# Hymba step on one core: a contiguous copy of the query for the residue blocks of two chunks, the last recurrence unit's first steps ahead of the scores, another order of tile pools, later merge turns

## The chip, the cores and the metric

The kernel runs on one core of a Trainium2 chip. The metric is the device time of one execution in microseconds (us), the median of several runs. A profiled execution of the same program gives the trace; its times are counted from its first instruction. TensorE is called PE (its weight loads PEld), VectorE DVE, ScalarE ACT, GpSimd POOL, and the queue that issues most DMAs SP.

## The reference, cut to what matters

One layer of a hybrid decoder over 2048 prompt tokens and 8x4 sample tokens, in float32:

```
a = rmsnorm(x);  [qa|fa|ia|ga|qb|kb|vb] = a @ w_in
h = x + concat(HGRN2(qa,fa,ia,ga), DilatedAttn(qb,kb,vb)) @ w_o
h = h + ConvFFN(rmsnorm(h))
h = h + sigmoid(rmsnorm(h) @ w_ple_gate) * (p @ w_ple_proj);   y = rmsnorm(h)
```

HGRN2 is a gated linear recurrence with 4 heads of 128: `S_t = diag(f_t) S_{t-1} + k_t v_t^T`, `o_t = S_t^T q_t`, then a per-head rmsnorm and a gate. The attention has 8 heads of 64; each query reads the last 129 positions of its sub-sequence for the dilations 1, 4 and 16 (windows 128, 512, 2048), and the three parts are put together by their softmax maxima and sums. The sample tokens do the same against a state and a cache of 2048 positions. The outputs are y for prompt and sample, the new states, and the caches.

## The kernel before, in words

The program is one long list of instructions that a tile framework puts in order: within each engine it orders by priority and by a simulated timeline, allocates the tiles, and sets the semaphores. Only PE in the attention stage runs in the order of the code (`manual_schedule`). Three stages follow each other.

**Projections** (0 to about 831 us). `in_phase` computes all of `a @ w_in` in two blocks of tokens; weights and tokens are split into a high and a low part, and each product is three matmuls (L344 to L346). The last group is the keys: each 128 tokens are scaled (L357), rotated (L318 to L321), turned by four transposes (L367), copied (L372) and stored in `kT_d`. Beside the second block, seven of the eight recurrence units run (`hgrn_unit`, two heads and 512 tokens each).

**Attention** (about 831 to 1212 us). Two generators are stepped in turns. `main` is `attn_phase`, `side` is `others()`: the eighth recurrence unit with `apart=True` (more yields), then the sample's attention, then the sample's recurrence. The loop at the end of the kernel steps `main` once a turn, and `side` once a turn up to turn 27 and every second turn later. A step is what lies between two `yield`s; what is stepped by `first` has a higher priority on the engines that the framework orders.

`attn_phase` goes over 4 head pairs p. For each it has two dilation groups: `di` 0 takes the tokens by residue mod 4 (a block is a chunk c of 512 tokens and a residue r), with keys of chunks 0 to c; `di` 1 takes 128 consecutive tokens, with their own and the previous 128 keys. Chunks have 4 blocks. A block of one or two key tiles is one *unit* of work for both heads, a block of three or four is two units. There are 40 units per pair and 160 in all. Pair 3 alternates the groups chunk by chunk. In turn x:

- `Unit.scores` of unit x: two matmuls per head (L797 with the high part of the keys `kH`, L798 with the low part `kL`), weights `lhsT` from `qS`, 128 columns. For `di` 0 these columns are every fourth element of `qS`, for `di` 1 they are consecutive. Keys of `di` 0 are 128(c+1) wide. The scores lie in one of two PSUM tiles `S`; DVE adds the mask and takes the minimum (L802), ACT takes the exponential (L803) into `P`.
- in every odd turn, `turned` for units x-3 and x-2 (transposes L810, copy L812 on DVE or ACT into `pt`) and `sums` for units x-7 and x-6 (`weighted`, matmuls with the values, L822; copy L872).
- what `at(x, ...)` has put down for the turn: `stage` (loads of q and k, L681, SP), `stack` (POOL rounds q, L148, and writes the rest of the rounding into the other half, L692; ACT copies k by residue, L695; POOL takes its rest, L696), `values_chunk` (L717, L720), and the steps of `merge`.

`merge` joins the two groups of a chunk: at +0 it loads statistics (L728), at +2 DVE takes a minimum (L736), POOL a difference (L737), ACT an exponential (L738); at +3 POOL and DVE (L740 to L743, a reciprocal on DVE at L742); at +4 PE transposes the coefficients (L746), ACT copies (L748), SP stores and loads them spread out (L749, L753); at +8 POOL multiplies (L758); at +9 DVE adds (L760; POOL for pair 3) and SP stores the result in `mix_d`.

`hgrn_unit`, in steps: loads and two products; the diagonal (L460 on PE, L461 on DVE); three double levels, each with operands (L469, L474, L476), products (L484) and results (L423, L496) head by head; the last level (L516); transposes (L529); the state (L541, L545) and the outputs (L552, L553); the norm (`rsqrt_small`, L100 to L105), its product (L567), and the final transposes (L574).

The tiles of the attention lie where the projections' tiles lay, so each waits for the last reader of what lay there. The pools are opened in the order `pps` (PSUM of `side`), then `a_d` (stage), `a_r` (`qS`, `kH`, `kL`), `a_w` (mask, values, `P`, `pt`, `cf`, `o0`, `o1`), `a_s`, and the PSUM pools of scores, sums and transposes.

**Trunk** (about 1212 us to the end): output projection, ConvFFN and embeddings, nearly all matmuls of three terms (L142 to L144).

Of the kernel before, what the change touches and what calls it, by code (L numbers as in the profile page):

```python
# [11 lines left out]
F32 = mybir.dt.float32  # L12
# [35 lines left out]
def hymba_step_kernel(ctx: ExitStack, tc: tile.TileContext, I: dict, O: dict):  # L48
# [44 lines left out]
    def f32(ap):  # L93
        return ap.bitcast(F32)
# [341 lines left out]
    def hgrn_unit(u, heads, S, ld, wk, sp, plv, po, pms, msk, apart=False):  # L436
# [99 lines left out]
        for i, h in enumerate(heads):  # L536
# [6 lines left out]
            for c in range(4):  # L543
                s = sp.tile([128, 128], F32, name=f"S{h}", bufs=6)
                V.scalar_tensor_tensor(s, chain[-1], t["D"][:, c:c + 1], pu[:, 128 * c:128 * c + 128],  # L545
                                       op0=ALU.mult, op1=ALU.add)
                chain.append(s)
# [15 lines left out]
        if apart:  # L563
            yield
        for i, h in enumerate(heads):
            o = st[h]["o"]
            V.tensor_mul(o, o, r[:, 4 * i:4 * i + 4].rearrange("p (c x) -> p c x", x=1).to_broadcast([128, 4, 128]))  # L567
        if apart:
            yield
        for i, h in enumerate(heads):  # L570
# [10 lines left out]
    def hgrn_sample(hp, pps):  # L581
# [13 lines left out]
        G.tensor_mul(E, q, f)  # L595
        yield
        at = hp.tile([NS, 4, NS], F32, name="hsat")
# [41 lines left out]
        ahead = [state_in(0), state_in(1)]  # L639
        yield  # L640
        for bb in range(8):
# [31 lines left out]
    def attn_phase(spare, rest):  # L673
# [11 lines left out]

        def stack(c, q, k):
            cs = slice(512 * c, 512 * c + 512)
            js = slice(128 * c, 128 * c + 128)
            split = "p (i r) -> p r i"
            for hh in range(2):  # L690
                round_g(qS[:, hh, cs], q[:, hh])
                G.tensor_sub(qS[64:, hh, cs], q[64:, hh], f32(qS[64:, hh, cs]))  # L692
            for hh in range(2):
                t = k[:, hh].rearrange(split, r=4)
                A.copy(kH[:, hh, :, js], t)  # L695
                G.tensor_sub(kL[:, hh, :, js], t, f32(kH[:, hh, :, js]))  # L696

        first = stage(0, 0, [t[:, :1024].rearrange("p (h t) -> p h t", h=2) for t in spare])
        yield
        dp, rp, wk, sm, pS, pA, pT = rest()  # L700


        qS = rp.tile([128, 2, SEQ], F32R, name="qS")
        kH = rp.tile([128, 2, 4, 512], F32R, name="kH")
        kL = rp.tile([128, 2, 4, 512], F32R, name="kL")
        mask = wk.tile([128, 768], F32, name="mask", bufs=1)
        SP.dma_start(mask, I["amask"])
        stack(0, *first)
        yield
# [16 lines left out]
        def merge(p, c, parts, both):  # L726
# [23 lines left out]

            cf = wk.tile([128, 2, 512], F32, name="cf", bufs=2)
            for h in range(2):
# [10 lines left out]
        class Block:  # L763


            def __init__(self, p, di, c, r):
                self.p, self.di, self.c, self.r = p, di, c, r
                self.pt = {}
                if di == 0:
                    self.q = lambda hh: qS[:, hh, 512 * c + r:512 * c + 512:4]  # L770
                    self.nk = c + 1
                    self.k = lambda t, hh: t[:, hh, r, :128 * c + 128]
                    self.v = [(n, r) for n in range(c + 1)]
                else:
                    b = 4 * c + r
                    self.q = lambda hh: qS[:, hh, 128 * b:128 * b + 128]
                    self.nk = 2 if b else 1
                    self.k = lambda t, hh: t[:, hh].rearrange("p r (n i) -> p n r i", i=32)[:, b + 1 - self.nk:b + 1]
                    self.v = [(x // 4, x % 4) for x in range(b + 1 - self.nk, b + 1)]
# [3 lines left out]
        class Unit:  # L783
# [5 lines left out]
            def scores(self, both):  # L789
# [4 lines left out]
                s = pS.tile([128, 512], F32, name="S")  # L794
                self.pe = wk.tile([128, 512], F32, name="P", bufs=6)
                for i, hh in enumerate(self.heads):
# [8 lines left out]
            def turned(self, on_act):  # L805
# [3 lines left out]
                for i in range(n):  # L809
                    PE.transpose(pt[:, i], self.pe[:, 128 * i:128 * i + 128], ident)  # L810
                out = wk.tile([128, 4, 128], F32, name="pt", bufs=8)
                (A.copy if on_act else V.tensor_copy)(out[:, :n], pt[:, :n])  # L812
# [33 lines left out]
        for p in range(4):  # L846
            for c in range(4):
# [6 lines left out]
                elif c:  # L854
                    at(x - 12, lambda c=c: staged.append(stage(0, c)))
                    at(x - 6, lambda c=c: stack(c, *staged.pop(0)))
                for di in range(2):
# [5 lines left out]
        def sums(u, x):  # L863
# [5 lines left out]
            if bl.r == 3:  # L869
                p, di, c = bl.p, bl.di, bl.c  # L870
                o = wk.tile([128, 512], F32, name=f"o{di}", bufs=5)
                A.copy(o.rearrange("p (i b) -> p b i", b=4) if di == 0 else o.rearrange("p (b i) -> p b i", b=4), acc)  # L872
# [4 lines left out]
                else:  # L877
                    merge_at([x + d for d in (0, 2, 3, 4, 8, 9)], p, c, (outs[c], o), bl.both)

        for x in range(n + 19):  # L880
            if x < n:
# [715 lines left out]
    S = []  # L1597
    for h in range(4):
        s = sp.tile([128, 128], F32, name=f"S{h}", bufs=6)
        G.memset(s, 0.0)  # L1600
        S.append(s)
# [3 lines left out]
    for x in in_phase(1, *args, plv, po):  # L1605
# [5 lines left out]
        else:  # L1611
            first(side, 2 if main else 1)
    first(side, 1000)
    in_st.close()
    pool = pools(attn_st)
    pps = pool("s_ps", 1, space=PSUM)
    rest += (pool("a_d", 2), pool("a_r", 1), pool("a_w", 3), pool("a_s", 3),
             pool("a_pS", 2, space=PSUM), pool("a_pA", 2, space=PSUM), pool("a_pT", 2, space=PSUM))
    step(main, 1)
# [12 lines left out]
    side = others()  # L1632
    with tc.manual_schedule(engines={mybir.EngineType.PE}):
        for turn in itertools.count(1):
            if not step(main, 1):
# [163 lines left out]
```

## Time and profile before

| | us |
|---|---|
| runs of the kernel before | 3019.55, 3015.72, 3021.38 (median 3019.55) |
| the profiled execution: its own time | 3014.84 |
| its span, first to last instruction | 3013.0 |
| PE busy in the span | 2926.5 (97%) |
| DVE, ACT, POOL busy | 2191.6 (73%), 1304.5 (43%), 667.9 (22%) |
| attention stage | about 831 to 1212 |

A row of a timeline has the start, the duration, the engine, the line, the operation, what it writes and reads, its shape and count, and in brackets how long the engine stood idle before it and what released it. Matmuls are pipelined, so the time between the starts of two of them says more than the duration of one. A row of the windows has the busy time of PE, PEld, DVE, ACT and POOL in a stretch, then the granted TensorE clock (1.00 is full), the busy share of the DMA engines, and GB/s. A row of the waits has who waited for whom, us in all, how often, and the longest.

### The profile page before, as it was taken

Reading aid. Unit: us, or ns where it says so; the run is one execution under the profiler, and the core shown is the slowest. Engines: PE = TensorE matmul, PEld = TensorE weight load, DVE = VectorE, ACT = ScalarE, POOL = GpSimd, SP = SyncE. Lnnn points to the kernel's source line nnn. Section 1 sums busy time; section 2 is a strip of 40 time slices with the busy share of each in tenths; the row PEclk is TensorE's granted clock in tenths of the full one; section 3 lists DMA queues with packets and bytes.
Section 4 is the critical chain, followed back from the end, with each engine's and each line's share of the span. In section 5 each row is a group of like instructions: output and inputs, shape, how many; then the busy total and the mean of one; then the engine's idle time right before and its main releaser. Section 6 shows DMA issues by size and latency. Waiting matters only on the chain.

```text
span 3013.0 us, 52001 instructions
## 1 busy us (share of the span) xinstructions
PE 2926.5 (97%) x18639; PEld 2738.0 (91%) x18639; DVE 2191.6 (73%) x4761; ACT 1304.5 (43%) x2824; POOL 667.9 (22%) x780
## 2 busy tenths in 40 slices
PE   8999999999978989999999999999999999999998
PEld 8977789987767667999999999999999999999997
DVE  7666868884466557568988889766769777777777
ACT  5333423231156665334444444544444544444443
POOL 1443222221134553102443431000001000000000
PEclk9999999999989999999999999999999999999999
DMA  5898533342248996766666568677778777778873
GB/s 174 311 337 309 198 103 110 104 134 95 91 115 243 303 246 194 260 225 222 227 209 194 191 198 300 231 250 252 245 231 311 242 245 244 257 248 290 272 274 131
DMA packets 328579, 664.08 MB, mean 220 GB/s; under 512 B 46400, under 2 KB 114112, under 8 KB 326528
## 3 DMA queue, kind: packets, MB, share of 16 engines
q1 hardware_dynamic: 291472, 472.65, 48.4%
q0 software_dynamic: 33264, 121.13, 12.6%
q10 hardware_dynamic: 3584, 66.98, 6.1%
q8 instruction: 147, 2.41, 0.3%
q14 instruction: 112, 0.92, 0.1%
HBM read 513.69 MB, written 213.92 MB: 241 GB/s over the span
## 4 chain that ended last, share of the span: by engine, by line
PE 72%; issue 9%; DVE 7%; DMA 7%; ACT 2%; POOL 2%; SPq 1%; DVEq 0%; POOLq 0%; ACTq 0%
PE mm L142 16%; PE mm L144 16%; PE mm L143 16%; PE mm L346 2%; PE mm L344 2%; PE mm L345 2%; PE lv L484 2%; PE acc L822 2%; PE S L797 1%; PE PT L810 1%; PE S L798 1%; DMA draw<-in_w_down_dram 1%; DMA xr<-in_xT_dram 1%; DVE h L1291 1%; DMA wd_d<-dw 1%
## 5 line engine op out<-in xcount | busy, mean ns | idle before, releaser
L143 PE MATMUL mm<-w 128*128 128x348 f32 (+3 forms) x3636 | 1166.1, 321 | 1.1 <-DVE w L1435 0.7
L142 PE MATMUL mm<-w 128*128 128x348 f32 (+3 forms) x3508 | 1109.7, 323 | 15.2 <-ACT s L1233 5.8
L144 PE MATMUL mm<-w 128*128 128x348 f32 (+3 forms) x3508 | 1117.4, 321 | 1.3 <-DVE w L181 1.3
L143 PEld LDWEIGHTS mm<-w 128*128 128x128 f32 x3636 | 684.3, 188 | 3.8 <-DVE w L1067 1.8
L142 PEld LDWEIGHTS mm<-w 128*128 128x128 f32 x3508 | 656.5, 188 | 23.6 <-ACT s L1233 8.5
L144 PEld LDWEIGHTS mm<-w 128*128 128x128 f32 x3508 | 659.0, 188 | 2.6 <-DVE w L181 1.8
L181 DVE TENSOR_TENSOR w<-raw,w 128x512 fp32r<-128x512 f32 x586 | 421.9, 725 | 170.3 <-ACT w L180 165.3
L180 ACT CAST w<-raw 128x512 fp32r<-128x512 f32 x586 | 360.6, 621 | 402.8 <-PE mm L144 293.1
L1275 POOL DMA_DIRECT2D w<-wd_d x231 | 123.8, 536 | 906.2 <-PE mm L144 800.6
L1291 DVE TENSOR_TENSOR h<-h,mm 128x348 f32<-128x348 f32 (+1 forms) x504 | 248.4, 509 | 45.9 <-PE mm L144 44.4
L803 ACT ACTIVATE P<-P,st 128x256 f32<-128x256 f32 (+3 forms) x256 | 134.1, 526 | 87.5 <-DVE st L802 85.9
L802 DVE CUSTOM_DVE_ANT_0 P<-S,mask 128x256 f32<-128x256 f32 (+3 forms) x256 | 105.0, 449 | 73.1 <-PE S L798 50.1
L1233 ACT COPY s<-mm 128x348 f32<-128x348 f32 (+1 forms) x198 | 87.9, 444 | 158.1 <-PE mm L144 157.8
L345 PE MATMUL mm<-wl,xh 128*128 128x512 f32 x352 | 140.7, 400 | 1.1 <-DVE wl L267 1.1
L344 PE MATMUL mm<-wh,xh 128*128 128x512 f32 x352 | 140.6, 403 | 0.0
L346 PE MATMUL mm<-wh,xl 128*128 128x512 f32 x352 | 140.3, 399 | 0.0
L142 PE MATMUL mm<-xh,wh 128*128 128x384 f32 (+2 forms) x384 | 125.7, 332 | 8.6 <-ACT xh L242 5.1
L143 PE MATMUL mm<-xl,wh 128*128 128x384 f32 (+2 forms) x384 | 126.9, 333 | 0.8 <-DVE xl L243 0.8
L144 PE MATMUL mm<-xh,wl 128*128 128x384 f32 (+2 forms) x384 | 125.5, 330 | 1.5 <-DVE wl L267 1.4
L267 DVE TENSOR_TENSOR wl<-wraw,wh 128x512 fp32r<-128x512 f32 x104 | 86.3, 851 | 34.0 <-POOL wh L148 28.9
L181 DVE TENSOR_TENSOR dw<-draw,dw 128x512 fp32r<-128x512 f32 x77 | 69.4, 909 | 55.8 <-ACT dw L180 55.0
L797 PE MATMUL S<-kH,qS 128*128 128x256 f32 (+3 forms) x256 | 97.7, 396 | 8.2 <-DVE st L802 7.3
(348 smaller groups left out, 5155.0 us busy)
## 6 DMA issues: line engine op xcount, KB each, us to landing
w<-wd_d POOLq DMA_DIRECT2D x231, 512.0 KB, 5.6
wd_d<-dw SPq DMA_DIRECT2D x77, 512.0 KB
out_sk_dram<-in_cache_k_dram ACTq DMA_DIRECT2D x56, 584.0 KB
out_sv_dram<-in_cache_v_dram ACTq DMA_DIRECT2D x56, 584.0 KB
raw<-in_w_gate_dram SPq DMA_DIRECT2D x110, 256.0 KB
raw<-in_w_up_dram SPq DMA_DIRECT2D x110, 256.0 KB
wraw<-in_w_in_dram SPq DMA_DIRECT2D x104, 256.0 KB
raw<-w_gate_d SPq DMA_DIRECT2D x88, 256.0 KB
```

The costliest lines, as they stand in the source:

```text
L142: PE.matmul(ps, lhsT=wh, rhs=xh, start=first, stop=False, skip_group_check=read)
L143: PE.matmul(ps, lhsT=wh, rhs=xl, start=False, stop=False, skip_group_check=read)
L144: PE.matmul(ps, lhsT=wl, rhs=xh, start=False, stop=last, skip_group_check=read)
L180: A.copy(w[:, 0], raw)
L181: V.tensor_sub(w[:, 1], raw, f32(w[:, 0]))
L344: PE.matmul(ps, lhsT=xh[k][:, js], rhs=wh, start=k == 0, stop=False)
L345: PE.matmul(ps, lhsT=xh[k][:, js], rhs=wl, start=False, stop=False)
L346: PE.matmul(ps, lhsT=xl[k][:, js], rhs=wh, start=False, stop=k == NK - 1)
L797: PE.matmul(s[:, w * i:w * i + w], lhsT=bl.q(hh), rhs=bl.k(kH, hh), start=True, stop=False)
L803: A.activation(pe, pe, AF.Exp, bias=mn, scale=-1.0, accum_out=st[:, bl.r, hh, 0:1])
L1275: G.dma_start(t, wd_d[p][n - 1])
L1291: V.tensor_add(o, o, acc[m][:, :H])
```

## The change

1. A new tile `q4` holds the query of chunks 0 and 1 ordered by residue. `stack` fills it with a DVE copy per head for c < 2, and the `di` 0 blocks of these chunks take their weights from it. Chunks 2 and 3 go on reading `qS` in steps of four.
2. For pair 0, the remainders of chunks 0 and 1 (two of q, two of k each) are computed by DVE instead of POOL.
3. Eight steps of `side` are taken ahead of the first turn. With `apart`, the recurrence unit has two more yields around its norm; the sample's recurrence has one more at its start and one less before its states. In all `side` has two more steps.
4. Pools are opened in another order: `a_r` (with `q4`), `a_w`, `a_d`, and a new `a_o` for `o0`, `o1` and `cf`; the PSUM of scores and sums comes before that of `side`.
5. Buffers: `S` of the recurrence 6 to 5, `P` 6 to 5, `pt` 8 to 6.
6. The merge's last three steps move from +4, +8, +9 to +8, +11, +12, and the loop has two more turns.

```diff
@@ hgrn_unit
-                s = sp.tile([128, 128], F32, name=f"S{h}", bufs=6)
+                s = sp.tile([128, 128], F32, name=f"S{h}", bufs=5)
...
         r = rsqrt_small(sp, v.rearrange("p h c -> p (h c)"), [128, 8])
         if apart:
             yield
+            yield
         for i, h in enumerate(heads):
             o = st[h]["o"]
             V.tensor_mul(o, o, r[:, 4 * i:4 * i + 4].rearrange("p (c x) -> p c x", x=1).to_broadcast([128, 4, 128]))
         if apart:
+            yield
             yield
@@ hgrn_sample
         G.tensor_mul(E, q, f)
-        yield
+        for _ in range(2):
+            yield
...
         ahead = [state_in(0), state_in(1)]
-        yield
@@ attn_phase
-        def stack(c, q, k):
+        def stack(c, q, k, E=G):
...
             for hh in range(2):
                 round_g(qS[:, hh, cs], q[:, hh])
-                G.tensor_sub(qS[64:, hh, cs], q[64:, hh], f32(qS[64:, hh, cs]))
+                E.tensor_sub(qS[64:, hh, cs], q[64:, hh], f32(qS[64:, hh, cs]))
+                if c < 2:
+                    V.tensor_copy(q4[:, hh, :, js], f32(qS[:, hh, cs]).rearrange(split, r=4))
             for hh in range(2):
                 t = k[:, hh].rearrange(split, r=4)
                 A.copy(kH[:, hh, :, js], t)
-                G.tensor_sub(kL[:, hh, :, js], t, f32(kH[:, hh, :, js]))
+                E.tensor_sub(kL[:, hh, :, js], t, f32(kH[:, hh, :, js]))
...
-        dp, rp, wk, sm, pS, pA, pT = rest()
+        dp, rp, wk, ok, sm, pS, pA, pT = rest()
         qS = rp.tile([128, 2, SEQ], F32R, name="qS")
+        q4 = rp.tile([128, 2, 4, 256], F32R, name="q4")
...
-        stack(0, *first)
+        stack(0, *first, V)
...
-            cf = wk.tile([128, 2, 512], F32, name="cf", bufs=2)
+            cf = ok.tile([128, 2, 512], F32, name="cf", bufs=2)
...
-                    self.q = lambda hh: qS[:, hh, 512 * c + r:512 * c + 512:4]
+                    self.q = lambda hh: (q4[:, hh, r, 128 * c:128 * c + 128] if c < 2 else
+                                         qS[:, hh, 512 * c + r:512 * c + 512:4])
...
-                self.pe = wk.tile([128, 512], F32, name="P", bufs=6)
+                self.pe = wk.tile([128, 512], F32, name="P", bufs=5)
...
-                out = wk.tile([128, 4, 128], F32, name="pt", bufs=8)
+                out = wk.tile([128, 4, 128], F32, name="pt", bufs=6)
...
-                    at(x - 6, lambda c=c: stack(c, *staged.pop(0)))
+                    at(x - 6, lambda c=c: stack(c, *staged.pop(0), V if c == 1 else G))
...
-                o = wk.tile([128, 512], F32, name=f"o{di}", bufs=5)
+                o = ok.tile([128, 512], F32, name=f"o{di}")
...
-                    merge_at([x + d for d in (0, 2, 3, 4, 8, 9)], p, c, (outs[c], o), bl.both)
+                    merge_at([x + d for d in (0, 2, 3, 8, 11, 12)], p, c, (outs[c], o), bl.both)
...
-        for x in range(n + 19):
+        for x in range(n + 21):
@@ the body
-        s = sp.tile([128, 128], F32, name=f"S{h}", bufs=6)
+        s = sp.tile([128, 128], F32, name=f"S{h}", bufs=5)
...
     pool = pools(attn_st)
+    ar, aw, ad, ao = pool("a_r", 1), pool("a_w", 3), pool("a_d", 2), pool("a_o", 5)
+    rest += (ad, ar, aw, ao, pool("a_s", 3), pool("a_pS", 2, space=PSUM), pool("a_pA", 2, space=PSUM))
     pps = pool("s_ps", 1, space=PSUM)
-    rest += (pool("a_d", 2), pool("a_r", 1), pool("a_w", 3), pool("a_s", 3),
-             pool("a_pS", 2, space=PSUM), pool("a_pA", 2, space=PSUM), pool("a_pT", 2, space=PSUM))
+    rest.append(pool("a_pT", 2, space=PSUM))
     step(main, 1)
...
     with tc.manual_schedule(engines={mybir.EngineType.PE}):
+        first(side, 1)
+        step(side, 7)
         for turn in itertools.count(1):
```

## The prediction

> **What bounds the kernel now.** I read the page first, then the windows of the attention stage, then its waits and timeline engine by engine, because everything the change touches lies there.
>
> ```profile
> span 3013.0 us, 52001 instructions
> PE 2926.5 (97%) x18639; PEld 2738.0 (91%) x18639; DVE 2191.6 (73%) x4761; ACT 1304.5 (43%) x2824; POOL 667.9 (22%) x780
> 840.00:860.00 20.00, 13.20 (x57) 11.84 (x55) 10.00 (x41) 12.54 (x30) 14.81 (x14) 0.63 1.01 256
> 860.00:880.00 20.00, 16.40 (x122) 14.42 (x122) 18.96 (x56) 12.03 (x35) 7.20 (x7) 1.00 0.23 54
> 920.00:940.00 20.00, 17.07 (x145) 13.99 (x145) 16.32 (x58) 14.58 (x43) 12.32 (x18) 0.84 0.95 316
> 940.00:956.00 16.00, 16.00 (x125) 12.14 (x121) 6.17 (x32) 9.74 (x32) 6.97 (x7) 1.00 1.09 270
> 1026.00:1050.00 24.00, 23.99 (x175) 18.09 (x174) 10.69 (x47) 13.36 (x45) 6.07 (x8) 0.93 1.08 275
> ```
>
> PE is the bound: only 86.5 us of the span are left to it, so a gain must come from PE's pauses in this stage, from stretches at a lower clock (0.63, 0.84), or from matmuls that take longer than they need. The last two windows hold the first two chunks of pairs 1 and 2: PE is full there, and DVE has 9.8 of 16 us free. Between 860 and 880 it is DVE that is full (18.96 of 20).
>
> **The query copy.** Start to start tells what a score matmul costs.
>
> ```profile
> 940.60 0.40 PE L797 MATMUL S<-kH,qS 128*128 128x128 f32 x1
> 940.83 0.40 PE L798 MATMUL S<-kL,qS 128*128 128x128 f32 x1
> 899.52 0.28 PE L797 MATMUL S<-kH,qS 128*128 128x128 f32 x1
> 899.64 0.27 PE L798 MATMUL S<-kL,qS 128*128 128x128 f32 x1
> 1038.39 0.39 PE L797 MATMUL S<-kH,qS 128*128 128x256 f32 x1
> 1038.62 0.40 PE L798 MATMUL S<-kL,qS 128*128 128x256 f32 x1
> 1194.87 0.29 PE L798 MATMUL S<-kL,qS 128*128 128x256 f32 x1
> 1194.99 0.29 PE L797 MATMUL S<-kH,qS 128*128 128x256 f32 x1
> ```
>
> The rows at 940 and 1038 have weights from every fourth element and follow at 0.23 us, at width 128 and at 256; those at 899 and 1194 have consecutive weights and follow at 0.12. The width doesn't matter, the step does: the weight load sets the pace, and `q4` saves 0.115 us a matmul. Chunks 0 and 1 have 4 residues x 2 heads x 2 key parts = 16 matmuls each, 32 a pair, 128 in all: 14.7 us, of which 3.7 belong to pair 0 (counted in the start below) and 11.0 to pairs 1 to 3. The Trainium skill says otherwise: "TensorE: Matmul & The Clock Gate", section "LDWEIGHTS (loading the stationary operand)", has a load time that depends on the number of columns alone; by that the copy would gain nothing, and the time would be 3011. The rows at one width differ in nothing but the step, so the measurement decides, and that case gets no chance of its own.
>
> Does PE keep the 11.0? The DMA engines are full in both windows (1.09, 1.08), and the sample's key loads already end last sometimes:
>
> ```profile
> PE s L928 <- DMA skt<-in_kT_d_dram: 5.1, 2, 2.8
> ```
>
> If these loads set the pace, the 7.4 us of pairs 1 and 2 come back as waits, and 3.7 are left. I take 8, between 3.7 and 11.0 and a little nearer to the upper end, since PE is at 16.00 of 16 and 23.99 of 24 in the two windows, with no wait for a DMA in them.
>
> The copy adds 16 DVE instructions of 128x512. No row shows DVE reading in steps of four; the nearest are DVE's copy of this size, and ACT's casts with and without the step.
>
> ```profile
> L812 DVE COPY pt<-PT 128x512 f32<-128x512 f32 x80 | 53.2, 683 | 2.4 <-PE PT L810 2.4
> L695 ACT CAST kH<-stage 128x512 fp32r<-128x512 f32 x30 | 32.7, 1140 | 21.3 <-DMA stage<-kT_d 16.5 <-PE S L797 4.7
> L180 ACT CAST w<-raw 128x512 fp32r<-128x512 f32 x6 | 3.2, 610 | 0.0
> ```
>
> So 0.68 us, or by ACT's ratio 1140/610 up to 1.28; I take 0.7, the same engine. That is 11 us of DVE time (up to 20). For pairs 1 to 3 it lies in DVE's free time; only its place in DVE's queue costs, below. I put 2 us on PE, between 0 and the rival's price.
>
> **The start (831 to 880).**
>
> ```profile
> 830.85 0.39 PE L346 MATMUL mm<-wh,xl 128*128 128x512 f32 x1
> 835.63 1.09 PE L367 MATMUL ms<-c_ident,ev 128*128 128x128 f32 x4 [3.95 <-DVE ev L321]
> 839.56 3.72 PE L460 MATMUL s<-hq,hF 128*128 128x128 f32 x16
> 847.72 0.50 PE L797 MATMUL S<-kH,qS 128*128 128x128 f32 x1 [4.44 <-DVE st L802]
> 859.23 0.89 PE L484 MATMUL s<-hM,hF 128*128 128x192 f32 x4 [1.64 <-DVE at L496]
> 865.87 1.84 PE L484 MATMUL s<-hM,hF 128*128 128x192 f32 x8
> 841.43 0.53 SPq L707 DMA_DIRECT2D mask<-in_amask_dram  x1
> 847.15 0.29 DVE L802 CUSTOM_DVE_ANT_0 P<-S,mask 128x128 f32<-128x128 f32 x1 [4.85 <-DMA mask<-in_amask_dram]
> 826.26 0.22 DVE L319 TENSOR_TENSOR rb<-ev,c_rope 128x64 f32<-128x64 f32 x1
> 832.52 1.30 DVE L319 TENSOR_TENSOR rb<-ev,c_rope 128x64 f32<-128x64 f32 x1
> ```
>
> Projections end at 831.2. The last rotation takes longer than the same line did six us earlier (1.30 for 0.22), and PE waits 3.95. Then the scores stop for the mask, issued on SP only at 841.43, landed at 847.15: PE idles 4.44 and its clock falls. With the pools by time of need, mask and `qS` lie where tiles are read before the very last matmul, so the mask no longer stands behind the second chunk's stage loads. The eight steps taken ahead are the diagonal and the first double level: L460 (3.72 at the low clock, about half at full), L484 for two heads (twice 1.84), with two PE waits of about 1.6 as at 859.23, and DVE's steps between: about 9 us of work that needs neither mask nor `qS`, its loads and operands being long there. They replace the pauses, and PE alone could gain 12 to 15 us.
>
> DVE can't. From 840 to 880 it has 29 us of work in 40 (10.00 and 18.96), and it gets eight remainders and four copies more, 12 x 0.7 = 8 us, a part of it before 840. Some 5 us stay free, and it can't be packed fully, since each L802 waits for scores. I take 5 for the start, pair 0's share of the copy included, with ends 0 and 10.
>
> **The norm of the unit.**
>
> ```profile
> 921.44 1.12 PE L574 MATMUL s<-c_ident,at 128*128 128x128 f32 x4 [5.10 <-DVE at L567]
> 913.52 1.47 DVE L101 TENSOR_SCALAR rs_y<-rs_i 128x8 int32<-128x8 int32 x1
> 920.29 0.17 DVE L104 SCALAR_TENSOR_TENSOR rs_t<-rs_t,o_v 128x8 f32<-128x8 f32 x1
> 907.80 1.20 POOL L148 TENSOR_SCALAR qS<-stage 128x512 fp32r<-128x512 f32 x2 [32.00 <-PE S L798]
> ```
>
> The norm is step 28, its transposes step 30: turns 28 and 32. With the extra yields the transposes are step 32, and with eight steps ahead these are turns 20 and 24: four turns apart as before. But turn 28 falls beside pair 1's `stack` (from turn 31), where POOL works after 32 idle us and DVE's small steps take 1.47 instead of 0.17. Turns 20 to 24 lie in POOL's idle stretch. Eleven steps at 0.2 end in about 2.5 us, the transposes no longer wait, and the 5.10 goes. In the window after it the clock is 0.84: 3 us lost in 20, half of which I count. Gain 6.5, ends 0 and 8.
>
> **The merge.**
>
> ```profile
> 1113.46 0.27 PE L746 MATMUL PT<-c_ident,w 128*16 128x128 f32 x1 [3.54 <-DVE pt L812]
> 1111.10 0.20 DVE L742 RECIPROCAL mn<-mn 128x8 f32<-128x8 f32 x1 [4.68 <-POOL mn L741]
> 1109.70 1.20 POOL L148 TENSOR_SCALAR qS<-stage 128x512 fp32r<-128x512 f32 x2 [5.54 <-DMA stage<-qT_d]
> ```
>
> The big wait at L746 comes from a late stage load: POOL stands at L148, POOL's steps of the merge stand behind it, DVE stands at L742, and the L802s behind that. ACT's cast of the same chunk's keys waits likewise. Of this chain only L746 moves; L742 stays at +3. The next scores and exponentials are as late as before, so I count 1 us, with ends 0 and 4. POOL's products three turns after the transposes instead of four meet their loads sooner; POOL mostly waits there anyway, at no cost.
>
> **Buffers.** Six `pt`, five `P` and five `S` hold exactly what is alive: `pt` of turn x takes the place of a unit summed in turn x-2, `P` that of one turned by x-2, and a state chain has five tiles. All were read on PE before. Cost 0; if a copy is late by a turn, it waits under one turn of PE work, about 2 us.
>
> **The end.** `side` has 94 steps instead of 92 and a lead of 8, so it ends some 12 turns earlier; its PE work isn't lost, only moved. The pair at the end is exposed:
>
> ```profile
> 1204.90 3.47 POOL L758 TENSOR_TENSOR o<-o,cf 128x512 f32<-128x512 f32 x2 [18.32 <-DMA cf<-coef_d]
> 1208.33 0.67 POOL L737 TENSOR_TENSOR w<-mn,st 128x16 f32<-128x16 f32 x1
> 1209.04 0.22 ACT L738 ACTIVATE w<-w 128x16 f32<-128x16 f32 x1 [3.03 <-POOL w L737]
> ```
>
> The last but one merge's L758 waits for its spread coefficients; behind it on POOL stands the last merge's L737, behind that on ACT L738 and a copy that PE's last sums need. With its transposes four turns later the coefficients come about 3 us later. Cost 2, ends 0 and 3.5.
>
> **Sum**, against the profiled execution's own 3014.84 us (span 3013.0): 8 + 5 + 6.5 + 1 - 2 - 2 = 16.5 us less, 2998.3. The median of the runs is 3019.55, 4.7 above that execution, so the sum is moved there: **3003**.
>
> **Rivals.**
>
> *All of it surfaces.* PE keeps 11, 10, 8 and 4, nothing is paid back: 33 us, 2986. For it speaks that every one of these pauses is on PE, the bound; against it DVE's 18.96 of 20 and the full DMA engines. 0.13.
>
> *The gain goes elsewhere.* DVE takes the start's gain (0), the DMAs leave 3.7 of the copy, the norm gives 5, and 2 + 3.5 are paid: about 3 us less, 3016, no change. The same comes out if the layout doesn't bring the mask forward, which the diff says nothing of in numbers. 0.16.
>
> *Slower: DVE stands behind POOL.* For pairs 1 to 3 the copy reads what POOL's L692 has just written, so it can't begin before, and POOL's L148 itself stands behind stage loads (5.54 above) and products that wait for coefficients (18.32). On DVE the L802s of two units stand behind the copy, PE has two `S` tiles, and stops after them. The row at 1111.10 shows the price where this happens: 4.68 on DVE, 3.54 on PE. At six places, with 2 us for the falling clock each, 33 us, against a gain of 18.5: 3034. It decides from DVE waits of about 2 us a place: between 920 and 940, where pair 1's stacks run, DVE has 3.7 us free in 20, and below that it is hidden. Against it speaks that most stacks found their loads there, 7.3 us of waits over 30 instructions:
>
> ```profile
> L148 POOL TENSOR_SCALAR qS<-stage 128x512 fp32r<-128x512 f32 x30 | 18.4, 632 | 45.4 <-PE S L798 33.1 <-DMA stage<-qT_d 7.3 <-PE acc L822 4.9
> ```
>
> A smaller form of it: copies and POOL's steps can shut each other out, as the two rows of L319 suggest, at 1.30 - 0.22 = 1.1 us for each of 16 copies, 17 us of DVE, which alone would bring the sum near the second rival. The Trainium skill says so: "SBUF — State Buffer", section "Who interferes with whom", has copies from SBUF to SBUF on VectorE in a mode that takes the pair of ports shared with GpSimd, and whoever comes later waits for the whole instruction. 0.11 for this rival.
>
> **The numbers.** Forecast 0.60, the others 0.13, 0.16, 0.11. A difference of 0.2%, 6 us, is about what a measurement of this kernel can tell. Faster by that is the forecast and the first rival: 0.73, and a little of the second: 0.74. Same 0.15, slower 0.11. The range takes the first rival's middle and the second's with some of its spread, 2986 to 3019; the slower rival and half of the first's spread are outside, about 0.2.
>
> **What would show it.** Right: score matmuls of chunks 0 and 1 at 0.12 start to start; L460 right after 831; the mask landed by 841; L574 without a wait near 890; the stage 12 to 20 us shorter; the trunk as long as before. Wrong: L802 idle behind the copies at pairs 1 to 3 by over 2 us each, waits for `skt` beyond 5.1 us by what the copy gained, or PE pauses in the block ahead as long as those it replaces (over 10 us before the first score).

## The result: slower by 0.6%, and the profile after

The changed kernel took 3037.06 us (median of 6 runs, 3028.89 to 3046.32) against 3017.68 for the kernel before (6 runs, 3014.23 to 3021.38): 1.0064 times as long, 95% interval 1.0046 to 1.0083. The forecast was 3003, with a range of 2986 to 3019. The profiled execution of the changed kernel is its fastest of the six, 3028.89 us, so its trace shows 14 of the 19 us. Four single runs in the later comparisons took 4654 to 12764 us, the longest that of the kernel with the copy and the late addition; they are counted in the medians given below, and not in the ratios.

The first lines of its page:

```profile
span 3027.1 us, 52015 instructions
...
PE 2915.4 (96%) x18639; PEld 2727.9 (90%) x18639; DVE 2207.6 (73%) x4785; ACT 1303.0 (43%) x2824; POOL 669.3 (22%) x772
```

PE has 111.7 us of the span without work, 25 more than before, and 11 us less busy time. The windows of the attention stage, first before, then after. The columns are the stretch, its length, busy time and instructions of PE, PEld, DVE, ACT and POOL, the granted clock, the DMA share and GB/s.

```profile
831.00:900.00 69.00, 53.40 (x360) 46.84 (x358) 49.55 (x150) 38.79 (x94) 30.03 (x28) 0.85 0.46 117
900.00:1000.00 100.00, 91.26 (x811) 70.59 (x810) 66.46 (x230) 65.44 (x202) 44.02 (x52) 0.97 0.88 256
1100.00:1212.00 112.00, 102.54 (x943) 83.92 (x941) 78.24 (x289) 68.95 (x216) 52.60 (x73) 0.95 0.69 189
```

```profile
831.00:900.00 69.00, 51.05 (x369) 45.20 (x367) 56.58 (x165) 41.66 (x110) 19.66 (x18) 0.88 0.46 119
900.00:1000.00 100.00, 85.80 (x751) 61.67 (x751) 58.82 (x203) 57.64 (x171) 37.17 (x44) 0.90 0.98 283
1100.00:1212.00 112.00, 95.53 (x868) 79.47 (x869) 79.82 (x295) 67.33 (x211) 59.03 (x77) 0.91 0.58 151
```

PE is busy for less of every window shown, and in the two from 900 and from 1100 on at a lower clock. The stretch between them, 1000 to 1100, is another case: PE gets through as many matmuls (812 against 814) in 87.70 us instead of 93.23, at 0.97 against 0.95. Before 831 both kernels run alike, and the trunk behind the stage is as long as before, only 13 to 14 us later. So the whole loss lies in the stage. PE's waits there, after (total us, times, longest):

```profile
PE s L934 <- DMA skt<-in_kT_d_dram: 12.1, 4, 4.8
PE s L971 <- DMA skt<-in_v_d_dram: 9.4, 3, 6.3
PE PT L816 <- ACT P L809: 6.2, 3, 4.4
PE S L803 <- DVE q L696: 5.0, 1, 5.0
PE s L484 <- POOL hM L476: 4.8, 1, 4.8
PE mm L142 <- ACT w L1072: 4.3, 1, 4.3
```

The sample's loads (tile `skt`), 5.1 us of waits before, now cost 21.5. All of PE's rows of this view from 820 to 1245 us add up to 65.8 us, against 41.4 before. The first score of each block tells where the time goes: counted from the start of the trace, the changed kernel is 2.7 us ahead at the first score of pair 1, 7.6 behind at that pair's second dilation group, 3.2 behind at the first score of pair 3, and 13.2 behind at the very last score. Pair 3 takes 89.9 us from first to last score; before it took 79.8. Both stretches in the windows, before and after:

```profile
1120.00:1200.50 80.50, 77.74 (x713) 65.53 (x710) 60.02 (x228) 47.20 (x160) 32.81 (x47) 0.98 0.69 194
```

```profile
1123.40:1213.30 89.90, 76.72 (x685) 64.54 (x683) 59.06 (x225) 51.05 (x164) 38.24 (x50) 0.89 0.55 148
```

A part of the reason is in SP's queue. The timeline of SP, before and after, at the stage loads of pair 3's last two chunks:

```profile
1093.04 0.61 SPq L681 DMA_DIRECT2D stage<-qT_d  x1
1103.06 0.60 SPq L681 DMA_DIRECT2D stage<-qT_d  x1
1103.76 1.23 SPq L681 DMA_DIRECT2D stage<-kT_d  x2
...
1111.42 2.12 SPq L681 DMA_DIRECT2D stage<-kT_d  x2
...
1125.56 0.38 SPq L979 DMA_DIRECT2D mix_d<-mixs  x1
```

```profile
1106.35 0.38 SPq L985 DMA_DIRECT2D mix_d<-mixs  x1
...
1112.01 1.72 SPq L637 DMA_DIRECT2D hs<-in_state_dram  x3
1113.83 1.26 SPq L683 DMA_DIRECT2D stage<-qT_d  x2
1115.19 1.22 SPq L683 DMA_DIRECT2D stage<-kT_d  x2
...
1118.48 1.35 SPq L683 DMA_DIRECT2D stage<-kT_d  x2
1120.21 4.45 SPq L725 DMA_DIRECT2D v<-v_d  x4
...
1126.03 0.38 SPq L733 DMA_DIRECT2D st<-stat_d  x1
```

SP issues one DMA behind the other: in the changed kernel the tile for the next queries is free at 1103.8 (below), and its load goes out at 1113.83, behind what stands ahead of it. Before, these eight loads go out between 1093 and 1113, and the sample's store of `mixs` and the recurrence's loads come behind them. After, the sample ends some 20 us earlier, and its store and the recurrence's eight loads stand ahead of the stage loads, which go out all eight together from 1113.8; values and the merge's statistics (L733) wait behind those.

The queue isn't all of it. Each of these loads needs a tile that held an earlier chunk, and POOL is done with the first chunk's queries 10.8 us later as well, at 1103.8 instead of 1093.0. The rows before and after:

```profile
1090.18 2.83 POOL L692 TENSOR_TENSOR qS<-stage,qS 64x512 fp32r<-64x512 f32 x2
```

```profile
1101.27 2.53 POOL L694 TENSOR_TENSOR qS<-stage,qS 64x512 fp32r<-64x512 f32 x2
```

Before, too, most of the loads went out some 10 us behind that or later. What the order on SP costs by itself is therefore shown by the runs below, not by these rows. What follows from the late loads, on the engines of the changed kernel:

```profile
1128.36 2.12 ACT L699 CAST kH<-stage 128x512 fp32r<-128x512 f32 x2 [2.19 <-DMA stage<-kT_d]
...
1130.08 0.18 DVE L741 TENSOR_REDUCE mn<-st 128x8 f32<-128x16 f32 x1 [6.52 <-DMA st<-stat_d]
...
1130.35 0.54 ACT L809 ACTIVATE P<-P,st 128x256 f32<-128x256 f32 x1
1131.03 1.66 PE L816 MATMUL PT<-c_ident,P 128*128 128x128 f32 x6 [4.37 <-ACT P L809]
1131.40 0.28 DVE L808 CUSTOM_DVE_ANT_0 P<-S,mask 128x128 f32<-128x128 f32 x1
```

ACT stands 2.19 us at the casts of the keys (L699) for their stage load, the exponentials stand behind the casts until 1130.35, and PE stands 4.37 us behind those. DVE stands 6.52 us at the merge for the statistics at the same time, but this wait of PE isn't for it: the first L808 behind the merge comes at 1131.40, when PE has gone on.

### The profile page after: what moved, and what is told of

Same layout as the page of the kernel before. It is cut to its first block, busy times and chain, and to the rows that moved or that the text cites. A ratio compares the mean times of both kernels' runs of the same rounds, so it can differ in the third digit from the quotient of the medians.

```text
span 3027.1 us, 52015 instructions
## 1 busy us (share of the span) xinstructions
PE 2915.4 (96%) x18639; PEld 2727.9 (90%) x18639; DVE 2207.6 (73%) x4785; ACT 1303.0 (43%) x2824; POOL 669.3 (22%) x772
## 4 chain that ended last, share of the span: by engine, by line
PE 77%; DMA 9%; DVE 8%; issue 2%; ACT 2%; POOL 1%; SPq 1%; DVEq 0%; POOLq 0%; ACTq 0%
PE mm L142 19%; PE mm L144 19%; PE mm L143 19%; PE mm L344 2%; PE mm L346 2%; PE mm L345 2%; PE lv L484 2%; DVE h L1297 1%; DMA skt<-in_v_d_dram 1%; PE acc L828 1%; PE PT L816 1%; DMA cf<-coef_d 1%; DMA draw<-in_w_down_dram 1%; PE S L803 1%; DMA skt<-in_kT_d_dram 1%
## 5 line engine op out<-in xcount | busy, mean ns | idle before, releaser
L808 DVE CUSTOM_DVE_ANT_0 P<-S,mask 128x256 f32<-128x256 f32 (+3 forms) x256 | 104.1, 448 | 61.7 <-PE S L804 50.2
L148 POOL TENSOR_SCALAR wh<-wraw 128x512 fp32r<-128x512 f32 x96 | 74.7, 791 | 123.9 <-DVE ev L300 41.4
```

The lines of the kernel that those rows point to most:

```text
L808: V.tensor_tensor_reduce(pe, s[:, w * i:w * i + w], bl.mask, 1.0, 3e38, ALU.add, ALU.min, mn)
```

## The experiments

Theory 1: the eight steps ahead bring the sample's 1 MB loads onto the border of pairs 0 and 1, where stage and value loads fill the DMA engines. Rivals: 2, the copies on DVE; 3, the merge's turns; and those that came up on the way. Each run is given as median and as ratio to the kernel before in the same comparison, with its interval. Waits and lengths of stretches come from one profiled execution of each kernel, which can lie up to 10 us off the median.

**Without the lead.** `first(side, 1)` and `step(side, 7)` taken out of the changed kernel.

> The changed kernel without the eight steps ahead of the scores; all else as changed. Theory 1 (the lead brings the sample's loads of 1 MB, 926.7 us before, 904.0 after, onto the stage and value loads at the border of pair 0 and pair 1, and PE waits for skt, 21.5 us against 5.1): the waits for skt fall to 7 us or less and the time to 3008 to 3018, below the kernel before by what the copy gains. Theory 2 (the copies on DVE, and DVE's L808 behind them, cost more than the copy gives): the time stays at 3030 or more, skt waits or not. Theory 3 (the merge's later turns: 6.5 us of DVE at the reduction of the statistics, 4.4 of PE behind it): 3030 or more too, with the wait of DVE for the statistics still there.

Measured 3021.49, ratio 1.0004 (0.9991 to 1.0017); skt waits 4.7 us. The loss is gone; the copy's gain doesn't show.

**The lead, with the sample at its old turn.**

```
+            for _ in range(6):
+                yield
             yield from attn_sample(...)
```

> The changed kernel with six empty steps between the unit of the recurrence and the sample's attention, so that the sample's first load is issued at the same turn as before while the unit still runs ahead. Theory 1: skt waits 7 us or less, time 3003 to 3015 (as without the lead, and the norm's 3 to 5 us less). Theories 2 and 3: 3030 or more. If the lead itself hurts in another way (the start, the clock), this stays above the kernel without the lead by over 8 us.

Measured 3019.66, ratio 1.0003 (0.9988 to 1.0018); skt waits 2.2 us. The first four loads still go out early (from 908.3 us; 926.7 before), other than the expectation says; from the fifth on the sample is where it was (940.3 against 947.9, the store of `mixs` at 1125.0 against 1125.6). With everything else as changed, the place of the sample's work alone makes the loss of 17 us. Copy, norm and lead together still gain nothing.

**The copy alone**, on the kernel before, with the smaller buffers.

> The kernel before with the query copy alone (remainders all on POOL, five S, five P, six pt to make room); no lead, old turns, old layout. Theory 1: 3005 to 3014, 4 to 12 us less than before, skt waits up to 9. Theory 2: 3025 or more, DVE's L802 idle behind the copies. Theory 3: 3018 or less.

Measured 3020.81, ratio 0.9999 (0.9986 to 1.0012); skt waits 13.0 us. Neither the gain nor the loss that was expected.

**The old merge turns** in the changed kernel: `(0, 2, 3, 8, 11, 12)` back to `(0, 2, 3, 4, 8, 9)`.

> The changed kernel with the merge's turns as before (0, 2, 3, 4, 8, 9); the lead stays. Theory 1: 3030 to 3040, skt waits above 15 us. Theory 2: the same. Theory 3: 3016 to 3024, DVE's wait for the statistics back to under 2 us and no 4.4 us of PE behind it.

Measured 3037.10, ratio 1.0050 (1.0032 to 1.0069). Theory 3 falls.

**Only the recurrence late**: the six empty steps between the sample's attention and its recurrence.

> The changed kernel with six empty steps between the sample's attention and the sample's recurrence: the sample's loads stay as early as in the changed kernel, its recurrence comes at the turns of before. Theory 1 (the loads meet the border of pairs 0 and 1): 3030 to 3040, skt waits above 12 us. Theory 4, new (the lead uses up the side work by turn 144 instead of 156, so that pair 3, whose scores are merged chunk by chunk, has fewer matmuls to lay beside its chain; PE pauses there and its clock falls: from the first to the last score of pair 3 89.9 us at 0.89 in the changed kernel, about 80 at 0.98 before): 3016 to 3024, pair 3 back to 80 to 85 us at 0.95 or more.

Measured 3034.44, ratio 1.0047 (1.0032 to 1.0062); skt waits 24.7 us, pair 3 92.5 us long. Theory 4 falls: the recurrence's matmuls come back to their old turns (the first one behind 424 score matmuls; 416 before, 376 in the changed kernel) and pair 3 is no shorter. On SP nothing has changed places: the store of `mixs` goes out at 1110.4, the stage loads behind it from 1117.9.

**Half loads.** Three kernels load two requests of each group of four and use them twice, so the scores and sums of the other two are left out:

```
-                    SP.dma_start(kt, I[src][4 * g:4 * g + 4, :, p]...)
+                    SP.dma_start(kt[:, :2], I[src][4 * g:4 * g + 2, :, p]...)
...
-                                  ... rhs=kt[:, bi],
+                                  ... rhs=kt[:, bi % 2],
```

> The kernel before with the sample's cached keys and values loaded for two of the four requests of a group alone, and used twice (the others' scores and sums are left out): the matmuls as many, the sample's DMA bytes half. It gives the level for the next two. If the loads bound PE before, 3008 to 3015, no skt waits; otherwise 3017 to 3021.

> The kernel before with the query copy alone and the same half loads of the sample. If the DMAs swallow what the copy gains on PE (13.0 us of skt waits with the copy, 5.1 without): 6 to 11 us below the kernel before with half loads. If DVE's queue swallows it: within 3 us of it.

> The changed kernel with the same half loads of the sample. Theory 1: within 5 us of the kernel before with half loads, or faster. Theory 4: 10 to 20 us slower than it, pair 3 still 87 us or more at a clock of 0.91 or less.

Measured: before with half loads 3014.32, ratio 0.9990 (0.9979 to 1.0000); with the copy 3019.21, 1.0000 (0.9988 to 1.0011); changed 3025.14, 1.0020 (1.0007 to 1.0033). Half the bytes take 12 us from the changed kernel and 3 to 5 from the one before. So a part of the loss is DMA load, but 9 to 11 us stay, in pair 3 (88.3 us); theory 1 is not enough. And without any skt wait the copy is 3 to 5 us slower: the waits for these loads are not what swallows its gain.

**The sample's end late**: the six empty steps ahead of its very last products.

```
             for si, src in enumerate(("v_w", "v_d")):
...
+            for _ in range(6 * g):
+                yield
             for bi in range(4):
```

> The changed kernel with six empty steps ahead of the very last products of the sample's attention: its loads stay as early as in the changed kernel, but its store to mix_d and the recurrence's loads come in SP's queue behind the stage loads of pair 3, as in the kernel before; in the changed kernel they stand ahead of them, and the eight stage loads of pair 3 are issued together at 1113.8 to 1118.5 us instead of spread over 1093 to 1111. Theory 5, new (that order on SP is the part of the loss that half loads did not remove, 11 us): stage loads of pair 3 spread again, pair 3 from 89.9 to 78 to 84 us, the time 3022 to 3029, the skt waits at pair 1 still there (over 10 us). Theory 1 alone: 3032 to 3040.

Measured 3025.16, ratio 1.0019 (1.0004 to 1.0034). SP's timeline and pair 3 in the windows:

```profile
1104.62 1.26 SPq L683 DMA_DIRECT2D stage<-qT_d  x2
1105.98 1.22 SPq L683 DMA_DIRECT2D stage<-kT_d  x2
...
1114.47 1.22 SPq L683 DMA_DIRECT2D stage<-kT_d  x2
1124.16 0.38 SPq L987 DMA_DIRECT2D mix_d<-mixs  x1
```

```profile
1119.80:1200.80 81.00, 73.05 (x710) 61.09 (x707) 59.32 (x229) 47.41 (x155) 37.98 (x55) 0.98 0.63 170
```

With the stage loads ahead of the sample's store again, pair 3 takes 81.0 us at 0.98, though the skt waits are still 15.6 us. The profiled execution is a quick one, 3015.59 us. The recurrence's matmuls come at the same turns here as in the kernel with only the recurrence late (3034.44, 1.0047); those two differ in the sample's last products and store, and so in the order on SP, and in 9 us. Some 12 of the 19 us hang on the sample's end, as theory 5 has it; the other 6 to 7 stay while its loads are early, and are gone where they stand at their old place (3019.66).

**The lead alone**, on the kernel before.

> The kernel before with the eight steps ahead of the scores and nothing else: no copy, old buffers, old turns, old layout, no extra steps in the recurrence. Theory 7, joined from theories 1 and 5 (the lead alone loses the time, by the sample's loads at the border of pairs 0 and 1 and by pair 3's stage loads behind the sample's end in SP's queue): 3032 to 3042, eight stage loads of pair 3 together, pair 3 over 86 us. If the loss needs the copy, the later merge or the layout beside it: 3015 to 3024.

Measured 3022.93, ratio 1.0008 (0.9998 to 1.0017). Theory 7 falls in this form: the stage loads stand together behind the sample's end here too (1109.4 to 1120.2), and the kernel is 10.4 us behind at the first score of pair 3, yet pair 3 takes 73.1 us and gives most of it back. So the early sample and the order on SP cost some 3 us by themselves; for the other 16 they need something else of the change beside them. That pair 3 is short because less side work is left there would fit, and isn't shown.

**The changed kernel without the copy.**

> The changed kernel without the query copy: lead, layout, buffers and merge turns as changed, pair 3's stage loads still behind the sample's end in SP's queue. Theory 9 (the lead alone is caught up in pair 3, 73 us there; the copy is what keeps the kernel from catching up, so lead and copy together make the loss): 3018 to 3026, pair 3 under 84 us. If the copy has no part in the loss: 3032 or more, pair 3 over 87 us.

Measured 3029.08, ratio 1.0030 (1.0016 to 1.0045), pair 3 85.9 us. Between both expectations: the copy is 8 to 10 of the 19 us when it stands beside the early sample. Some 6 us more than with the lead alone stay, with layout, buffers, two more steps and the merge's turns; these weren't taken apart further.

**The copy under other covers.** The merge's addition on DVE three turns later, `(0, 2, 3, 4, 8, 12)`, with and without the copy; then the same with half loads.

> The kernel before with the query copy, and the merge's last step (the addition on DVE) three turns later than before (0, 2, 3, 4, 8, 12). Theory 6 (what the copy gains on PE is lost where DVE stands at the addition for POOL's products, which wait for the spread coefficients: 6.80 us on DVE and 4.98 on PE behind it in the copy with half loads): 5 to 10 us below the next kernel, DVE's waits at the addition under 2 us in all. If it is DVE's time for the copies: within 3 us of the next one.

> The kernel before with the addition three turns later and nothing else, the level for the one above. By theory 6: 3015 to 3020, since before waits only 8.1 us there on DVE, most of it hidden.

> The query copy, half loads of the sample (the other half of its scores and sums left out) and the late addition, all three on the kernel before. Theory 8 (the copy's gain is swallowed by whichever of two covers is still there, the sample's loads or DVE at the merge's addition): 6 to 11 us below the next kernel. If DVE's own time for the copies (14 us more of DVE in the stage) swallows it: within 3 us of the next, or above.

> Half loads of the sample and the late addition on the kernel before, no copy: the level for the one above. 3012 to 3016, as with half loads alone, by theory 8 as by the other.

Measured: 3020.66 with the copy (1.0007, 0.9994 to 1.0019) against 3019.42 (1.0004, 0.9991 to 1.0016); with half loads 3021.81 (1.0007, 0.9996 to 1.0017) against 3015.08 (0.9986, 0.9976 to 0.9996). Theories 6 and 8 fall as far as this edit can tell: the turn at which the addition is asked for isn't where it runs. The timelines of SP, POOL, DVE and PE with copy, half loads and late addition:

```profile
942.20 0.35 SPq L752 DMA_DIRECT2D coef_d<-wt  x1
...
951.61 1.11 SPq L756 DMA_DIRECT2D cf<-coef_d  x2
...
959.40 2.48 POOL L761 TENSOR_TENSOR o<-o,cf 128x512 f32<-128x512 f32 x2 [9.27 <-DMA cf<-coef_d]
961.92 0.69 DVE L763 TENSOR_TENSOR o<-o,o 128x512 f32<-128x512 f32 x1 [7.06 <-POOL o L761]
963.00 1.97 PE L814 MATMUL PT<-c_ident,P 128*128 128x128 f32 x8 [5.24 <-DVE pt L816]
```

Between the coefficients' store and the load that spreads them lie 9.4 us on SP: it issues stage, key and value loads, and at the end waits 3.7 us for the store itself to land. Without the copy (half loads, late addition) the chain is as long: the store at 941.53, the load at 950.49, POOL at 958.22. But there DVE doesn't wait at the addition (961.59), nor PE behind it. With the copy PE comes to the last scores of pair 1's second chunk sooner (957.1 against 958.4, though it began 1.8 us later), and then waits 5.24 us for a chain that is as late as ever.

**The copy on POOL**: `G.tensor_copy` for `V.tensor_copy`.

> The kernel before with the query copy on POOL instead of DVE. If the copies' time on DVE (0.6 to 1.7 us each, 14 us in all) and their place in its queue swallow the gain: 3010 to 3016. If the gain is lost elsewhere (merge, DMAs), 3017 to 3024. If POOL gets too long a queue (its products for the merge later): above 3024.

Measured 3029.66, ratio 1.0033 (1.0018 to 1.0049). POOL's queue is the worse place: PE waits 8.3 us for `q` itself and 6.9 for the merge's weights, which POOL makes.

**The sample's loads spread**: one empty step behind each group of four loads but the seventh, seven in all; and the same without the copy.

> The changed kernel with seven empty steps spread through the sample's attention, one behind each group of four loads: the sample starts as early as in the changed kernel and ends as late as in the kernel before. Theory 7: pair 3's stage loads spread again and pair 3 78 to 84 us, skt waits under 12 us since the loads come 7 steps in 39 slower: 3012 to 3022. If an early start is bad at any rate: 3024 or more.

> The changed kernel without the query copy, with the sample's loads spread by seven empty steps: a version to beat both kernels. Theory 9, and the copy's record so far (0 to 7 us slower where it was added): 3010 to 3016, at or below the version with spread loads and copy. If the copy gains once the loads are out of its way: 3018 to 3024.

Measured 3017.11, ratio 0.9988 (0.9976 to 1.0000), and 3019.29, ratio 0.9995 (0.9978 to 1.0012). The sample can start early if it goes slowly and ends late: 20 us better than the changed kernel, skt waits 5.1 us. It is the best kernel here, but 3 us less than before is within what can be told from no change. Without the copy it is not better, so no harm of the copy shows there; expected was a gain of leaving it out. The kernel without the copy also warns against reading the length of pair 3 as a sign of late stage loads: they go out early there, from 1091.0 to 1108.5, the first score of pair 3 is 7.7 us earlier than before, and pair 3 still takes 88.2 us.

## Why the prediction was wrong, point by point

**The step that failed** is "The end": "it ends some 12 turns earlier; its PE work isn't lost, only moved", at a cost of 2. It priced the matmuls of the side work and the last merge, and not the side work's DMAs, which it had weighed only against the copy's gain: 32 loads of 1 MB, the store of `mixs` and the recurrence's eight loads, moved past pair 1's and pair 3's stage loads in SP's queue. With the sample back in its old place the changed kernel is where the kernel before is (3019.66). Part of the loss is DMA load, part is the order on SP: against their own levels half loads take 8 to 10 of the 19 us, the late end 12 to 14. The lead alone, with the same early sample and the same order, loses some 3; of what the rest of the change adds to it, the copy's part is measured, 8 to 10, and where some 6 come from stays open.

That accounts for the loss. The other half of the miss is that the gains, 20.5 us before the two costs, don't come out even with the sample in its old place. Term by term:

**The query copy, 8.** The size of the saving is right, in the timeline of the changed kernel:

```profile
1123.69 0.27 PE L803 MATMUL S<-kH,q 128*128 128x128 f32 x1
1123.81 0.27 PE L804 MATMUL S<-kL,q 128*128 128x128 f32 x1
1123.92 0.28 PE L803 MATMUL S<-kH,q 128*128 128x128 f32 x1
```

Start to start is 0.11 to 0.12 instead of 0.23. The argument that PE keeps it failed: "PE is at 16.00 of 16 and 23.99 of 24". Over the stage, with the copy alone:

```profile
831.00:1212.00 381.00, 331.07 (x2918) 254.97 (x2916) 261.82 (x889) 238.24 (x698) 180.91 (x210) 0.93 0.79 219
```

PE is busy 9.4 us less than before (340.43) in the same time, and its named waits are 50.9 us instead of 41.4. Six pairs of kernels differ in the copy (the first four also in the buffers that make room for it); the medians are those given above, with 3020.3 for the kernel before beside the copy alone, and PE's waits are the sum of its rows in the view of waits, 820 to 1245 us, of one execution each:

| beside | time without | with | PE's waits without | with |
|---|---|---|---|---|
| the kernel before | 3020.3 | 3020.8 | 41.4 | 50.9 |
| half loads | 3014.3 | 3019.2 | 39.8 | 53.0 |
| late addition | 3019.4 | 3020.7 | 46.6 | 50.3 |
| both | 3015.1 | 3021.8 | 42.2 | 54.6 |
| change, loads spread | 3019.3 | 3017.1 | 39.1 | 54.1 |
| the change | 3029.1 | 3037.1 | 49.8 | 65.8 |

The last two rows put kernels of different comparisons side by side; by the ratios the copy is 2 us faster in the one and 10 slower in the other. In each row PE waits 4 to 16 us longer with the copy. A stretch without a pause was read as PE setting the pace; in these rows the time saved comes back as waits, and where the timeline was followed above, PE met a chain through SP, the DMA engines, POOL and DVE. Pair 2's first chunk went from 11.1 us to 7.7 with the copy alone, and its third from 21.5 to 25.0. The Trainium skill warns of this: "Perfetto Trace Analysis", section "Identifying the Most-Contended Engine", calls the busy share of matmuls no good measure of how close TensorE is to its peak, and section "Optimization Strategy" says that the most contended engine can change over time. The traces agree: PE was busy for 16.00 of 16 us in such a stretch, and 9.4 us less of its work in the stage left the time as it was. Which one wait swallows the copy's gain, or whether it is always the next, isn't settled: taking away half the loads, asking for the addition later, or moving the copies to POOL didn't free it.

**DVE's price for the copy, 2, and the slower rival.** The rival's time, 3034, came near, its mechanism didn't: DVE waited 2.4 us in all for POOL at the copies, not two at each of six places. Its smaller form did happen. The changed kernel's copies in all, then from its timeline a copy while POOL has nothing to do, and POOL's remainders with a copy beside them:

```profile
L696 DVE CAST q<-qS 128x512 fp32r<-128x512 f32 x16 | 17.7, 1114 | 2.4 <-POOL qS L694 2.4
...
837.41 0.61 DVE L696 CAST q<-qS 128x512 fp32r<-128x512 f32 x1
...
1006.53 2.52 POOL L694 TENSOR_TENSOR qS<-stage,qS 64x512 fp32r<-64x512 f32 x2
...
1007.84 1.71 DVE L696 CAST q<-qS 128x512 fp32r<-128x512 f32 x1 [0.16 <-POOL qS L694]
```

Of the 16 copies the shortest took 0.61 us, the middle one 0.93, the longest 1.96; 17.7 us in all, where 11 were taken and up to 20 allowed for. The Trainium skill's rule in "SBUF — State Buffer", section "Who interferes with whom", that such copies and GpSimd can shut each other out for a whole instruction, fits these rows: POOL's second remainder ends at 1009.05, and the copy that began beside it 0.5 us later, 1.1 us more than by itself.

**The start, 5.** The mask was no longer waited for, as forecast, and L460 had even run before 831. But PE's pauses in the block ahead were as long as those they replaced:

```profile
838.17 0.42 PE L803 MATMUL S<-kH,q 128*128 128x128 f32 x1 [5.03 <-DVE q L696]
848.31 0.38 PE L803 MATMUL S<-kH,q 128*128 128x128 f32 x1 [2.89 <-DVE st L808]
854.14 2.90 PE L484 MATMUL s<-hM,hF 128*128 128x192 f32 x8 [4.81 <-POOL hM L476]
```

Between 831 and 860 DVE is busy for 25.43 of 29 us, before for 14.42. That is the second rival's "DVE takes the start's gain". Eight steps of side work were done in the same time, a gain that should have come out at the end of the stage. With the lead alone pair 3 was short (73.1 us), though that kernel isn't faster either (3022.93); in the changed kernel pair 3 was long.

**The norm, 6.5.** Right at its place, given back in the next stretch. The 5.10 us at the transposes became 1.99 (at 901.13), and the clock between 920 and 940 rose from 0.84 to 1.00, while between 900 and 920 it fell from 0.99 to 0.91. But the changed kernel's next two windows read:

```profile
920.00:940.00 20.00, 18.18 (x185) 13.23 (x185) 12.99 (x55) 15.81 (x50) 14.00 (x19) 1.00 1.08 289
940.00:960.00 20.00, 15.73 (x153) 12.25 (x151) 11.54 (x44) 13.10 (x42) 7.09 (x10) 0.83 1.07 286
```

PE waits 1.82 us for skt in the first and 4.11 in the second, and the clock falls to 0.83 there, where before PE was busy for 20.00 of 20 at 1.00.

**The merge, 1.** The wait of 3.54 us at L746 went (0.6 at most at L751); a stall of 4.37 at L816 came in its place, behind ACT's casts and their late stage loads. The later turns as such change nothing (3037.10 with the old ones).

**Buffers, 0**, were not tried by themselves; together with the copy they cost nothing that can be told (3020.81).

Of the signs that the prediction named for being wrong, two came true: the waits for skt went from 5.1 to 21.5, and the pauses in the first block stayed (12.7 us in its three rows, 10.0 in those of the prediction that they replace), though not all of them ahead of the first score.

## What to carry to other kernels

When work is moved, list what it issues on every queue, DMAs first, and look which loads it passes: some 12 of these 19 us came back when one store and the loads behind it stood behind a later pair's loads on SP again. Don't take a stretch in which PE is full as proof that a matmul made faster gains time; here it gained none in any of six pairs beyond what can be told, so ask what PE will wait for at the end of the stretch. In the changed kernel an early start of the background loads cost nothing only where their rate was lowered as well.

## What the runs showed of the hardware

DVE's copy that reads every fourth element of 4 bytes takes 0.61 us at 128x512 when POOL is idle. Its plain copy of that size took 0.68, but reads PSUM, so the two don't tell what the step costs. ACT's cast with the same step took 1.14 against 0.61. On PE the step in the weights doubles the distance of matmuls, 0.23 against 0.11 to 0.12. Pauses come with a lower clock behind them: in pair 3 PE was without work for 13.2 us of 89.9, against 2.8 of 80.5 before, and the granted clock was 0.89 instead of 0.98.
